# Branch A of an encoder layer: head outputs stored by SyncE, and both merge portions behind a step's second scores

## The chip, the cores and the metric

One core of one Trainium2 chip runs the whole layer. The metric is device time in microseconds for one execution. The kernel before takes 1680.21 us, the median of three runs from 1679.45 to 1682.18.

## The reference, cut to what matters

There are 1280 tokens of 1024 features in float32: a sample of 1024 and a prompt of 256, which do not attend to each other. A projection gives queries, keys and values of two attention branches, and gate logits. Branch A has eight query heads over two key heads and a window of 128 to either side, with a sink in the softmax. Branch B has twelve heads in three groups of dilation 1, 4 and 16, and merges the groups per head by the softmax over their log-sums:

```python
outs.append(_from_residues(o, dil))
lses.append(_from_residues(lse, dil))
alpha = jax.nn.softmax(jnp.stack(lses), axis=0)
o = jnp.sum(alpha[..., None] * jnp.stack(outs).astype(jnp.float32), axis=0)
...
merged = gates[:, :, 0] * (o_a.reshape(b, S, A_Q) @ w_branch_a) + gates[:, :, 1] * (o_b @ w_branch_b)
x = x + merged @ w_out
h = _rmsnorm(x, g_mlp)
return x + jnp.square(jax.nn.relu(h @ w_up)) @ w_down
```

## The kernel before, in words

Large products run on TensorE (PE) as three passes of split float32 operands (`mm3`, L192, and the schemes that use L347). The stages follow each other: projection with branch B's attention beside it, branch A's attention, the gated products of the branches, the output projection, the MLP.

The change lies in branch A's stage, which is written for a manual schedule: each engine executes its instructions in the order in which the code issues them. It works on 4 units (`u`, two heads each) of 10 token tiles (`t`, 128 rows). `order` lists the 40 pairs of unit and tile, and the loop at L1426 takes two of them at each step, so `j` runs 0, 2, ..., 40. A step holds, in this order:

- `values_of` for the pair of tiles of two steps ago: PE multiplies values by probabilities into the one bank `pv` (L1205), VectorE (DVE) copies it to a tile `o` (L1208), of which there are **two buffers**, and the tile is stored to a DRAM scratch `scr_o` (L1209).
- `transposes` of the last step's probabilities: PE (L1189), evicted by ScalarE (ACT, L272) and DVE (L274).
- `scores` of the first tile: PE writes both heads into the two `sc` banks (L1163, L1164), DVE adds the bias and takes the maximum (L1165, then L1169). One portion of `fill`. The exponential of both heads on ACT (L1175).
- `scores` of the second tile, two portions of `fill`, and its exponential.

`fill` is the generator `logits`: PE's gate-logit products of the projection, which have nothing to do with attention. Its results go through ACT to a tile `gs` (L1230) and by a store of SyncE (SP) to DRAM (L1231). A cycle of it takes five steps, which is ten tiles, so that steps whose `j` differ by ten hold the same widths of tiles and the same products.

`merges` is the generator `merge`: the softmax over branch B's groups. Its **first portion** (before the loop) transposes the log-sums, stores them to DRAM and loads them back in another layout: 25 small DMAs, all issued by GpSimd (POOL; L1260 and L1277). Portions two to five are empty. **Portion six**, in the step with `j = 8`, is seven DVE instructions (L1283 to L1290). Portion seven is one exponential on ACT (L1292). **Portion eight**, with `j = 10`, is nine DVE instructions (L1294 to L1307) and six DMAs of POOL (L1310). Portion nine is empty, ten and eleven issue loads `r` on SP, three DMAs each (one L1326, two L1329), and each of the last eighteen issues one such load, two items ahead, and the products of its own item on POOL (L1345, L1348).

Two kinds of queue matter. POOL executes its DMA issues in order among its products. SP does nothing but issue DMAs, in order: an issue waits for what fills or frees its tile, and, since the program gives SP's DMAs eight completion semaphores in turn, for the landing of the DMA eight issues before it. SP's other DMAs here are the loads of the next unit (`kk`, `kp`, `q`, `qp`: L429 to L447), weights (`raw`, L222), the stores of `gs`, and after the loop the gates `sg` (L1479) and the stored heads (L1386).

Of the kernel before, what the change touches and what calls it, by code (L numbers as in the profile page):

```python
# [97 lines left out]
def encoder_kernel(  # L98
# [5 lines left out]
    nc = tc.nc  # L104
# [31 lines left out]
    def bank(tag, name=None):  # L136
        return psum.tile([P, 512], F32, name=name or tag, tag=tag, bufs={"mm": 3, "sc": 2, "pt": 2, "pv": 1}[tag])
# [81 lines left out]
    def fetch():  # L219
        src, shape, _ = specs[len(raws)]  # L220
        raws.append(wslot("raw", shape))
        nc.sync.dma_start(raws[-1], src)  # L222
# [58 lines left out]
    scr_o = [dram.tile([P, 4, 2, P], F32, name=f"scr_o{t}") for t in range(0, NT, 2)]  # L281
# [41 lines left out]
    def steps_of(gen, n):  # L323
        for _ in range(n):
            next(gen, None)
# [93 lines left out]
    def load_unit(u):  # L419

        st = {}
        g = u // 2
        if u == 0:
            shared["kp"] = slot("kp", (P, 4, NP), F32R)
        if u % 2 == 0:
            kk = [slot("kk", (P, NS), F32R) for _ in range(2)]
            for i in range(2):
                for r in HALVES:
                    nc.sync.dma_start(kk[i][r, :].bitcast(F32), scr_ka[g, i, :, :NS])  # L429
                    nc.sync.dma_start(shared["kp"][r, 2 * g + i, :].bitcast(F32), scr_ka[g, i, :, NS:])  # L430
            shared["k"] = [Pair(kk[i], shared["kp"][:, 2 * g + i, :]) for i in range(2)]
        st["q"] = [Pair(slot("q", (P, NS), F32R), None) for _ in range(2)]
        for h in range(2):
            nc.sync.dma_start(st["q"][h].s.bitcast(F32), scr_qa[u][h].rearrange("a d t -> (a d) t")[:, :NS])
        if u:
            load_prompt(u, st)
        else:
            shared["v"] = [slot("va", (P, 8, P)), None]
            nc.sync.dma_start(shared["v"][0],
                              scr_v[:NS, 512 : 512 + P].rearrange("(t p) c -> p t c", p=P))  # L440
        st["k"], st["v"] = shared["k"], shared["v"]
        return st
# [9 lines left out]
    def load_bias(u, make):  # L452
        b = make("bias", (P, 2, 3 * P))
        nc.gpsimd.dma_start(b, toeplitz(0, 3 * P, -P, 2 * u))
        return b
# [26 lines left out]
    def attention_b(make):  # L482
# [148 lines left out]
        for j in range(0, n + 4, 2):  # L631
            load_v(j)
            load_v(j + 1)
            if j < n:
                scores(j)
            load(j + 3)
            if j > 2:
                pv = values_of(j - 4)
                store_values(j - 4, (nc.vector, nc.scalar)[j // 2 % 2], *pv)
            if j < n:  # L640
                biased(j)
            if 0 < j <= n:
                transposes(j - 2, nc.scalar)
            if j < n:
                biased(j + 1)
            if 0 < j <= n:
                transposes(j - 1, nc.vector)
            load(j + 4)
            if j < n:
                exponentials(j)  # L650
                exponentials(j + 1)
            yield
# [487 lines left out]
    if True:  # L1140
# [4 lines left out]
        def a3(name, shape=(P, 2, 3 * P), n=3, dt=F32):  # L1145
            return att.tile(list(shape), dt, name=name, tag=name, bufs=n)
# [8 lines left out]
        def scores(u, t):  # L1155
            st, bias = units[u]
            lo, W, c0 = tiles[t]
            s = a3("s", n=3)
            m = small.tile([P, 2], F32, name="m", tag="m")
            for h in range(2):  # L1160
                ps = bank("sc")
                q = st["q"][h][:, P * t : P * t + P]
                nc.tensor.matmul(ps[:, :W], q, st["k"][1][:, P * lo : P * lo + W], start=True, stop=False)  # L1163
                nc.tensor.matmul(ps[:, :W], q, st["k"][0][:, P * lo : P * lo + W], start=False, stop=True)  # L1164
                nc.vector.tensor_tensor_reduce(  # L1165
                    s[:, h, :W], ps[:, :W], bias[:, h, c0 : c0 + W], 1.0, -3.0e38,
                    op0=ALU.add, op1=ALU.max, accum_out=m[:, h : h + 1],
                )
            nc.vector.scalar_tensor_tensor(nm_a[:, 2 * u : 2 * u + 2, t], m, -1.0, nsink[:, 2 * u : 2 * u + 2],  # L1169
                                           op0=ALU.mult, op1=ALU.min)  # L1170
            live[u, t] = s

        def exponential(u, t, h):
            W, s = tiles[t][1], live[u, t]
            nc.scalar.activation(s[:, h, :W], s[:, h, :W], AF.Exp, bias=nm_a[:, 2 * u + h : 2 * u + h + 1, t],  # L1175
                                 accum_out=l_a[:, 2 * u + h : 2 * u + h + 1, t])

        def transposes(u, t):

            pt = a3("pt", (P, 12, P), 1)  # L1180
            jobs, at = [], []
            for i in range(2):
                at.append(len(jobs))
                jobs += [(live[u, t + i], b, h) for b in range(tiles[t + i][1] // P) for h in range(2)]
            for i, tag, eng in ((0, "pt", nc.scalar), (4, "pt", nc.vector), (8, "mm", nc.scalar)):
                if i < len(jobs):
                    ps, e = bank(tag, "pt"), min(len(jobs), i + 4)
                    for k, (s, b, h) in enumerate(jobs[i:e]):
                        nc.tensor.transpose(ps[:, P * k : P * k + P], s[:, h, P * b : P * b + P], ident)  # L1189
                    moved(eng, pt[:, i:e, :], ps[:, : P * (e - i)].rearrange("p (i q) -> p i q", q=P))  # L1190
            for i in range(2):
                live[u, t + i] = pt, at[i]

        def values_of(u, t):

            pv = bank("pv")
            for i in range(2):
                lo, W, _ = tiles[t + i]
                pt, at = live.pop((u, t + i))
                v, rest = units[u][0]["v"]  # L1200
                for b in range(W // P):
                    k = lo + b
                    src = v[:, k, HALVES[u // 2]] if k < 8 else rest[:, k - 8, HALVES[u // 2]]
                    for h in range(2):
                        nc.tensor.matmul(pv[HALVES[h], P * i : P * i + P], src, pt[:, at + 2 * b + h, :],  # L1205
                                         start=b == 0, stop=b == W // P - 1, skip_group_check=True)
            o = a3("o", (P, 2, P), 2)
            nc.vector.tensor_copy(o, pv[:, : 2 * P].rearrange("p (i q) -> p i q", i=2))  # L1208
            nc.gpsimd.dma_start(scr_o[t // 2][:, u], o)  # L1209

        def sums_a():

# [153 lines left out]
    if True:  # L1366
# [5 lines left out]
        def high_b(b):  # L1372

            ob_hi.block(b)
            ob_lo.block(b)
            nc.scalar.activation(ob_hi.t[b, 0], merged[b], AF.Copy)

        def low_b(b):
            nc.vector.tensor_tensor(ob_lo.t[b, 0], merged[b], ob_hi.t[b, 0].bitcast(F32), op=ALU.subtract)
# [3 lines left out]
        def load_o(t):  # L1383
            if t % 2 == 0:
                rows_o[t] = slot("o", (P, 4, 2, P))
                nc.sync.dma_start(rows_o[t], scr_o[t // 2])  # L1386
# [34 lines left out]
        n = len(order)  # L1421
        fill = logits()
        merges = merge()
        next(merges)
        steps_of(fill, 2)
        for j in range(0, n + 2, 2):  # L1426
            if j > 2:
                values_of(*order[j - 4])
                if j < n:
                    next(merges, None)  # L1430
            if j:
                transposes(*order[j - 2])
            if j < n:
                scores(*order[j])
                next(fill)
                for h in range(2):
                    exponential(*order[j], h)
                scores(*order[j + 1])
                steps_of(fill, 2)
                if j > 2:  # L1440
                    next(merges, None)
                for h in range(2):
                    exponential(*order[j + 1], h)
            else:
                steps_of(fill, 2)
                next(merges, None)
            if j == n - 4:
                high_b(0)
                low_b(0)
            if j < n and order[j][1] == 0 and order[j][0] < 3:  # L1450
                u = order[j][0] + 1
                units[u] = load_unit(u), load_bias(u, lambda name, shape: a3(name, shape, 2))
            if j in (n - 6, n - 4):
                fetch()
            if j == n - 2:
                load_o(0)
                load_o(1)
# [51 lines left out]
        for i, (x, b, c) in enumerate(jobs):  # L1509
            t0, n = BLOCKS[b]  # L1510
# [528 lines left out]
```

## Time and profile before

| | us |
|---|---|
| the profiled execution, its own time | 1681.2 |
| its span on the core | 1679.4 |
| median of the three runs | 1680.21 |
| PE busy | 1664.9 (99%) |
| DVE busy | 953.6 (57%) |
| ACT busy | 716.3 (43%) |
| POOL busy | 513.3 (31%) |
| granted TensorE clock, mean | 0.999 |

Times in the trace are microseconds from the start of the span. A row of a timeline gives the start, the duration, the engine, the line, the operation with its tiles and the count; in brackets stands how long the engine had been idle before it, and what ended that. Branch A's loop takes the time from about 539 to 677. A row of the DMAs gives the line's tiles, the issuing queue, the count, the KB of each and the median time from issue to landing. PE's busy share counts matmuls with overlapping, modelled ends; what tells of the loss is the idle time and the spacing of starts.

### The profile page before, as it was taken

To read this page: it belongs to the slowest core of one execution; us is meant where nothing else is said; L and a number is where in the kernel's file an instruction comes from. 1 tells how busy PE (TensorE), PEld (TensorE's weight loads), DVE (VectorE), ACT (ScalarE), POOL (GpSimd) and SP (SyncE) were. 2 spreads that over 40 slices of the span, in tenths; PEclk is the share of its full clock that TensorE was granted. 3 is DMA by queue.
4 is the path that set the end of the run, shared out by engine and by line. 5 is a ranking of instruction groups with operands and counts; after the bars stand their busy time and mean duration, and the time that the engine had idled before them with its cause. 6 is when DMAs were issued, how large, how long until landed. Compare 5 with 4: busy or idle time off the path is not lost. (4 is left out here: it accounts for less than half of the span.)

```text
span 1679.4 us, 24840 instructions
## 1 busy us (share of the span) xinstructions
PE 1664.9 (99%) x9268; PEld 1414.1 (84%) x9268; DVE 953.6 (57%) x1535; ACT 716.3 (43%) x1476; POOL 513.3 (31%) x400
## 2 busy tenths in 40 slices
PE   9999999999999999999999999999999999999998
PEld 7898888888888888888888888888888888888886
DVE  6732233445554565677278545545556775867665
ACT  6232323345654556654176333333334333333445
POOL 1312222111112473200100646546455250614240
PEclk9999999999999999999999999999999999999999
DMA  7416562666667693845121443443356934733333
GB/s 249 151 57 127 133 135 74 162 190 194 192 186 225 182 255 110 296 133 201 38 89 59 160 155 109 136 160 119 121 190 227 363 101 134 259 101 116 119 119 125
DMA packets 222360, 262.45 MB, mean 156 GB/s; under 512 B 29568, under 2 KB 151216, under 8 KB 222240
## 3 DMA queue, kind: packets, MB, share of 16 engines
q1 hardware_dynamic: 214080, 239.80, 45.1%
q0 software_dynamic: 7872, 20.54, 5.5%
q8 instruction: 73, 1.20, 0.3%
q10 hardware_dynamic: 288, 0.52, 0.1%
q14 instruction: 47, 0.39, 0.1%
HBM read 175.13 MB, written 90.92 MB: 158 GB/s over the span
## 5 line engine op out<-in xcount | busy, mean ns | idle before, releaser
L347 PE MATMUL dn<-dhi,ulo 128*128 128x512 f32 x448 | 174.5, 389 | 0.1
L347 PE MATMUL dn<-dlo,uhi 128*128 128x512 f32 x448 | 174.3, 389 | 0.0
L347 PE MATMUL dn<-dhi,uhi 128*128 128x512 f32 x448 | 174.3, 389 | 0.0
L347 PE MATMUL x<-chi,wlo 128*128 128x512 f32 x424 | 166.7, 393 | 0.2 <-ACT c L1953 0.2
L347 PE MATMUL x<-clo,whi 128*128 128x512 f32 x424 | 165.7, 391 | 0.1
L347 PE MATMUL x<-chi,whi 128*128 128x512 f32 x424 | 165.1, 389 | 0.0
L314 DVE TENSOR_TENSOR wlo<-ta,whi 128x1024 fp32r<-128x1024 f32 x30 | 55.8, 1861 | 171.5 <-ACT whi L312 171.5
L314 DVE TENSOR_TENSOR wlo<-raw,whi 128x1024 fp32r<-128x1024 f32 x60 | 89.1, 1485 | 103.5 <-ACT whi L312 101.4
L393 POOL TENSOR_TENSOR tb<-raw 128x512 f32<-128x512 f32 x25 | 32.6, 1304 | 364.4 <-DMA raw<-in_w_in_dram 129.0
L347 PEld LDWEIGHTS dn<-dhi,ulo 128*128 128x128 f32 x448 | 84.1, 188 | 18.2 <-DVE ulo L186 0.5
L347 PEld LDWEIGHTS dn<-dlo,uhi 128*128 128x128 f32 x448 | 84.1, 188 | 17.5
L347 PEld LDWEIGHTS dn<-dhi,uhi 128*128 128x128 f32 x448 | 84.1, 188 | 17.4
L347 PEld LDWEIGHTS x<-chi,whi 128*128 128x128 f32 x424 | 79.6, 188 | 16.9
L1733 POOL TENSOR_TENSOR t<-raw,t 128x1024 f32<-128x1024 f32 x16 | 46.3, 2915 | 155.3 <-DMA raw<-in_w_down_dram 155.3
L347 PEld LDWEIGHTS x<-chi,wlo 128*128 128x128 f32 x424 | 79.8, 188 | 15.7 <-ACT c L1953 0.6
L347 PEld LDWEIGHTS x<-clo,whi 128*128 128x128 f32 x424 | 79.8, 188 | 15.1 <-DVE clo L314 0.4
L186 DVE TENSOR_TENSOR ulo<-uraw,uhi 128x1024 fp32r<-128x1024 f32 x56 | 88.5, 1602 | 3.5 <-ACT uhi L185 3.5
L1882 DVE TENSOR_TENSOR v<-v,dn 128x512 f32<-128x512 f32 x90 | 59.4, 682 | 41.2 <-PE dn L347 41.2
L1982 POOL TENSOR_TENSOR u<-u,u 128x640 f32<-128x640 f32 x16 | 25.1, 1568 | 173.0 <-ACT u L1900 173.0
L186 DVE TENSOR_TENSOR dlo<-raw,dhi 128x1024 fp32r<-128x1024 f32 x32 | 49.1, 1558 | 46.5 <-ACT dhi L185 45.6
L347 PE MATMUL dn<-dhi,up 128*128 128x512 f32 x224 | 73.5, 389 | 0.0
L185 ACT ACTIVATE dhi<-raw 128x1024 fp32r<-128x1024 f32 x32 | 33.5, 1058 | 92.8 <-PE dn L347 92.4
(325 smaller groups left out, 4685.0 us busy)
## 6 DMA issues: line engine op xcount, KB each, us to landing
scr_u<-u SPq DMA_DIRECT2D x112, 320.0 KB, 2.6
uraw<-scr_u SPq DMA_DIRECT2D x56, 512.0 KB, 4.3
raw<-in_w_down_dram SPq DMA_DIRECT2D x36, 512.0 KB, 6.1
raw<-in_w_up_dram SPq DMA_DIRECT2D x32, 512.0 KB, 5.4
raw<-in_w_in_dram SPq DMA_DIRECT2D x25, 512.0 KB, 5.1
sg<-scr_g SPq DMA_DIRECT2D x32, 256.0 KB, 6.3
uraw<-scr_u SPq DMA_DIRECT2D x28, 256.0 KB, 4.5
qk<-scr_kb SPq DMA_DIRECT2D x48, 128.0 KB, 2.9
```

Source lines behind the costliest of these rows:

```text
L185: nc.scalar.activation(hi, src, AF.Copy)
L186: nc.vector.tensor_tensor(lo, src, hi.bitcast(F32), op=ALU.subtract)
L314: nc.vector.tensor_tensor(lo, src, hi.bitcast(F32), op=ALU.subtract)
L347: nc.tensor.matmul(ps, a, b, start=first and i == 0, stop=last and i == len(seq) - 1, skip_group_check=True)
L393: (nc.vector if vector else nc.gpsimd).tensor_tensor(o, x, y, op=ALU.subtract)
L1733: nc.gpsimd.tensor_tensor(o, a, b, op=ALU.subtract)
L1882: nc.vector.tensor_tensor(v, v, ps, op=ALU.add)
L1982: nc.gpsimd.tensor_tensor(u[S1], u21, u22, op=ALU.add)
```

## The change

The store of a pair's output goes from POOL's queue to SP's. A merge portion no longer stands between `values_of` and `transposes`; both portions of a step now stand behind the second scores and their two portions of `fill`, ahead of the second exponential. Numbers and sizes of instructions stay as they were.

```diff
             o = a3("o", (P, 2, P), 2)
             nc.vector.tensor_copy(o, pv[:, : 2 * P].rearrange("p (i q) -> p i q", i=2))
-            nc.gpsimd.dma_start(scr_o[t // 2][:, u], o)
+            nc.sync.dma_start(scr_o[t // 2][:, u], o)
...
             if j > 2:
                 values_of(*order[j - 4])
-                if j < n:
-                    next(merges, None)
             if j:
                 transposes(*order[j - 2])
...
                 steps_of(fill, 2)
                 if j > 2:
-                    next(merges, None)
+                    steps_of(merges, 2)
                 for h in range(2):
                     exponential(*order[j + 1], h)
```

On DVE, at the step with `j = 8`: before, the seven instructions of portion six (those on `cb`) follow the copy of the output and stand ahead of the eviction `pt` and of all of the step's scores (`s,m<-sc,bias`).

```order
L1169 SCALAR_TENSOR_TENSOR nm_a<-m,nsink 128x2
L1208 COPY o<-pv 128x256
L1283 COPY cb<-cb 128x2x32
L1283 COPY cb<-cb 128x2x8
L1283 COPY cb<-cb 128x2x32
L1283 COPY cb<-cb 128x2x8
L1288 TENSOR_TENSOR cb<-cb 128x40
L1289 TENSOR_TENSOR cb<-cb 128x40
L1290 TENSOR_TENSOR cb<-cb 128x120
L274 COPY pt<-pt 128x512
L1165 ISA s,m<-sc,bias 128x256
```

In the changed kernel the same seven follow the second tile's scores, and the next instruction is the copy of the next step's output.

```order
L1165 ISA s,m<-sc,bias 128x256
L1165 ISA m 128x1
L1169 SCALAR_TENSOR_TENSOR nm_a<-m,nsink 128x2
L1283 COPY cb<-cb 128x2x32
L1283 COPY cb<-cb 128x2x8
L1283 COPY cb<-cb 128x2x32
L1283 COPY cb<-cb 128x2x8
L1288 TENSOR_TENSOR cb<-cb 128x40
L1289 TENSOR_TENSOR cb<-cb 128x40
L1290 TENSOR_TENSOR cb<-cb 128x120
L1208 COPY o<-pv 128x256
L274 COPY pt<-pt 128x512
```

So they moved past the eviction and all of the step's scores. Portion eight moves in the same way one step later.

On POOL, between the first portion's loads and portion eight's stores (`scr_c`), the first four output stores are gone; `bias` is the next unit's bias.

```order
 L1277 DMA cb<-scr_n 128x2x4 x2
 L454 DMA bias<-wide_1311 128x2x384
-L1209 DMA scr_o_91<-o 128x256
-L1209 DMA scr_o_92<-o 128x256
-L1209 DMA scr_o_93<-o 128x256
-L1209 DMA scr_o_94<-o 128x256
 L1310 DMA scr_c<-cb 128x32
```

Before, the first of them could only be issued when POOL was through with all of the first portion.

On SP, behind the third unit's queries (`q`, `qp`), where the merge's loads `r` begin: the stores of outputs five and six (`scr_o_95`, then `scr_o_91` of the next unit) now stand among the loads, and the stores of `gs` come ahead of a step's loads.

```order
 L434 DMA q<-scr_qa_114 128x1024 x2
 L447 DMA qp<-scr_qa_114 128x256 x2
+L1209 DMA scr_o_95<-o 128x256
+L1231 DMA scr_g_141<-gs 128x512
 L1326 DMA r<-scr_b_83 128x512
 L1329 DMA r<-scr_c 64x512 x2
-L1231 DMA scr_g_141<-gs 128x512
 L1326 DMA r<-scr_b_85 128x4x128
 L1329 DMA r<-scr_c 64x4x128 x2
+L1209 DMA scr_o_91<-o 128x256
+L1231 DMA scr_g_141<-gs 128x256
```

Every output store is now one of the DMAs that SP's eight semaphores count.

## The prediction

> **What bounds the kernel now.** The page comes first: which engine is full.
>
> ```profile
> PE 1664.9 (99%) x9268; PEld 1414.1 (84%) x9268; DVE 953.6 (57%) x1535; ACT 716.3 (43%) x1476; POOL 513.3 (31%) x400
> ```
>
> PE is idle for 14 us of 1679 at most, so a change that takes no work from PE can only win where PE waits. The second view is the waits of PE between 530 and 700, which takes in branch A's stage; it has one row.
>
> ```profile
> PE sc L1163 <- DVE m L1165: 2.6, 2, 1.8
> ```
>
> Two waits, 2.6 us in all, and both are for DVE to free a bank `sc`. PE's timeline shows where: at 566.9 to 568.8 (step `j = 8`) and at 575.1 to 575.8 (step `j = 10`), ahead of the second scores of the very steps that hold portions six and eight of the merge.
>
> ```profile
> 568.75 0.38 PE L1163 MATMUL sc<-kp,qp 128*128 128x256 f32 x1 [1.84 <-DVE m L1165]
> ...
> 575.83 0.44 PE L1163 MATMUL sc<-kk,q 128*128 128x384 f32 x1 [0.74 <-DVE m L1165]
> ```
>
> DVE's timeline tells why DVE was late.
>
> ```profile
> 557.46 0.42 DVE L1208 COPY o<-pv 128x256 f32<-128x256 f32 x1 [0.27 <-PE pv L1205]
> ...
> 566.26 0.42 DVE L1208 COPY o<-pv 128x256 f32<-128x256 f32 x1 [4.52 <-DMA scr_o<-o]
> 566.61 0.50 DVE L1283 COPY cb<-cb 128x64 f32<-128x64 f32 x4
> ...
> 567.68 0.68 DVE L274 COPY pt<-pt 128x512 f32<-128x512 f32 x1
> ...
> 573.07 0.27 DVE L1294 TENSOR_TENSOR cb<-cb 128x120 f32<-128x120 f32 x1
> ...
> 574.75 0.68 DVE L274 COPY pt<-pt 128x512 f32<-128x512 f32 x1
> ...
> 579.72 0.42 DVE L1208 COPY o<-pv 128x256 f32<-128x256 f32 x1 [2.00 <-PE pv L1205]
> ...
> 593.57 0.42 DVE L1208 COPY o<-pv 128x256 f32<-128x256 f32 x1 [0.27 <-PE pv L1205]
> ...
> 600.43 0.42 DVE L1208 COPY o<-pv 128x256 f32<-128x256 f32 x1 [2.11 <-PE pv L1205]
> ...
> 612.71 0.42 DVE L1208 COPY o<-pv 128x256 f32<-128x256 f32 x1 [1.52 <-PE pv L1205]
> ```
>
> The third output's copy (566.26) does not wait for PE, as the others do, but for the landing of an earlier output's store: there are two buffers `o`, and the first store had not landed. Why not, POOL's timeline says.
>
> ```profile
> 555.51 6.06 POOL L1277 DMA_DIRECT2D cb<-scr_n  x8 [0.29 <-issue]
> ...
> 562.27 1.15 POOL L1209 DMA_DIRECT2D scr_o<-o  x2
> ```
>
> POOL issued the merge's small loads until 561.6 and only then the first two output stores, the first of which belongs to the copy one step ahead of that at 557.46. So the first stall is the store's place in POOL's queue plus portion six on DVE (566.61 to 567.68, 1.07 us); the second is portion eight alone (573.07 to 574.75, 1.68 us).
>
> **The change part by part.** *The two stalls.* What they cost is best read from equal work. Copies at 557.46 and 579.72 bracket the steps with `j` from 6 to 12; those at 593.57 and 612.71 bracket `j` from 16 to 22, with the same widths of tiles and the same pieces of `fill`. The first stretch takes 22.26 us, the second 19.14. The difference, **3.12 us**, is 0.54 more than the idle time of 1.84 + 0.74, because modelled ends hide part of a wait. I take 3.12.
>
> *The store.* On SP the first store can go when its copy is done, one step ahead of 557.46: nothing but a store of `gs` stands near it on SP. The third copy is due at 564.32 (557.46 plus 6.86, which is 600.43 - 593.57, the same step ten later), two steps after the first, and the longest landing quoted below, 10.9 us, is under two steps. So the wait of 4.52 goes. POOL's twenty issues of some 0.57 us (1.15 for two) go too; POOL is not waited for in the stage, so I count nothing.
>
> *Portion six behind the second scores.* DVE then has 1.07 us of it between the second maximum and the next copy, where DVE waits for PE anyway: the bracket of 2.00 at 579.72 is such a gap. But ACT's exponential of the merge and then the second tile's exponentials queue behind it.
>
> ```profile
> 571.43 0.50 ACT L1175 ACTIVATE s<-s,nm_a 128x256 f32<-128x256 f32 x1
> ```
> ```profile
> 572.61 1.09 PE L1189 MATMUL pt<-ident,s 128*128 128x128 f32 x8
> ```
>
> The second tile's exponentials end at 571.93 here, and would end at most 1.07 us later against PE, as if at 573.00. PE's eight transposes start at 572.61 and take the first tile's four first; at an eighth of 1.09 - about 0.12 - each, the fifth falls near 573.06. So it just holds, and costs nothing; without that cover, up to half a us.
>
> *Portion eight behind the second scores.* 1.68 us into a DVE gap of 2.00: nothing. Its six stores and all later loads `r` come up to a step later for POOL, whose products nobody in the stage waits for.
>
> *The stores among SP's loads.* This is the price. Here SP's loads are queued up, and each issue needs the landing of the one eight before. SP's timeline and the DMA view of 580 to 582 give both routes at the same moment:
>
> ```profile
> 580.52 0.32 SPq L1326 DMA_DIRECT2D r<-scr_b  x1
> ```
> ```profile
> r<-scr_b SPq DMA_DIRECT2D x1, 256.0 KB, 10.9
> ...
> scr_o<-o POOLq DMA_DIRECT2D x1, 128.0 KB, 9.1
> ```
>
> The store is the fifth output's, and took POOL 9.1 us. On SP, issued just ahead of the load at 580.52, it takes at most that load's 10.9 and lands by 591.4. The seventh copy needs that buffer: it stands at 593.57 now, and at 590.45 with the 3.12 gone. So it would be up to 0.95 us late. What DVE's lateness costs PE is read from the stalls: at `j = 10`, 1.68 us cost 0.74 of idle time and its part of the hidden 0.54, some 0.9; at `j = 8`, 1.94 (566.26 - 564.32) and 1.07 cost the other 2.2. Both leave **0.8 us of lateness free**. The bounds of this term: nothing (it lands as fast as POOL's did) to some 3 us (first rival). I take 0.2, near the lower end, since 0.95 - 0.8 is what the row of the same moment gives.
>
> At that moment POOL's route was 1.8 us quicker than SP's. The Trainium skill has a rule that speaks against the move: by "DMA: Bandwidth & Descriptors", section "Queues, rings and completion order", a data engine takes turns between the rows of queues that have work, so a store in POOL's own row need not stand behind SP's backlog, and one in SP's row must. The trace agrees in sign, by those 1.8 us; were the rule the whole story, the sum would be the first rival's.
>
> *After the loop.* The last stores now stand ahead of SP's loads of the gates.
>
> ```profile
> 676.64 0.42 DVE L1208 COPY o<-pv 128x256 f32<-128x256 f32 x1 [0.39 <-PE pv L1205]
> ```
> ```profile
> 679.84 1.34 ACT L1484 ACTIVATE sg<-sg,bg 128x512 f32<-128x512 f32 x2
> ...
> 687.07 0.60 ACT L1230 ACTIVATE gs<-mm 128x512 f32<-128x512 f32 x1 [3.92 <-PE mm L192]
> ```
> ```profile
> sg<-scr_g SPq DMA_DIRECT2D x7, 256.0 KB, 4.7
> ```
>
> The first gate can be loaded after the copy at 677.06, less 3.12: 673.9, plus an issue and 4.7 us, 679.1. The sigmoid stood at 679.84, less 3.12: 676.7. It is 2.4 us late, and ACT has 3.92 us idle before the third `gs`; no PE bank waits. Nothing; without cover, under 2.4.
>
> **The sum** against the profiled execution's own time: 1681.2 - 3.12 + 0.2 = 1678.3. The median of the runs shown lies 1.0 below that execution, so 1680.21 - 2.9 = **1677.3**. A measurement of this kernel tells about 0.2% from no change, 3.36 us: the forecast lies just inside it.
>
> **The rivals.** *Stores caught in SP's backlog.* If a store takes the 10.9 us of SP's fullest moment wherever the next unit's queries are loaded, the tenth store counts most. POOL's timeline, DVE's, and the landing of the tenth store:
>
> ```profile
> 616.87 0.56 POOL L1209 DMA_DIRECT2D scr_o<-o  x1
> ```
> ```profile
> 626.71 0.42 DVE L1208 COPY o<-pv 128x256 f32<-128x256 f32 x1 [0.21 <-PE pv L1205]
> ```
> ```profile
> DMA to landing us min/median/max: 7.5/7.5/7.5
> ```
>
> It lands at 616.87 + 10.9 = 627.8 in place of 624.4 (POOL's, 7.5); the twelfth copy, now 626.71, would be due at 623.6. That is 4.2 late, less 0.8: 3.4 us back at the worst, and 0.15 at the fifth. So between 1 us and all of the gain goes back: 1678 to 1680.5, at the middle 1679.3. For it: SP's landings grow where POOL's grow. Against it: POOL's own 7.5 us there already holds the backlog, and by it the store is only 0.8 late. Chance 0.22. (The rule of the Trainium skill named above would make this the rule.)
>
> *SP's queue falls behind, and the kernel is slower.* With eight landings outstanding and 10.9 us each, SP issues one DMA in 1.36 us. If SP is bound by this count and not by bytes, the six stores added from the fifth to the tenth put SP 8.2 us back: the tenth lands at 632.6, the twelfth copy is 9.0 late, PE 8.2, net 8.2 - 3.1 = 5.1 slower, 1685.3. It decides from where that store lands after 627.5 (623.6 + 0.8 + 3.1). Against it: the bytes are the same as before, and a backlog bound by bytes does not grow by their changing queue. Chance 0.08.
>
> *The second exponential is late at `j = 8`*, since its cover is under 0.1 us at the worst: up to half a us back beside the 0.2, 1677.8. Chance 0.08.
>
> *The wait was not the store's place*, and the third copy stays late: only portions six and eight are cured. Then 1.94 us of lateness less 0.8 stays, and 3.12 - 1.14 = 2.0 is won: 1678.2. Against it: the copy's own row names `scr_o<-o` as what ended its idle time. Chance 0.02.
>
> **How the numbers follow.** The forecast has the remaining 0.60; with the scatter of the runs (1679.45 to 1682.18) its own range is 1676 to 1678.5. The range for 8 in 10 is 1675.9 to 1681.0: it takes in the first rival and the late exponential and leaves out the slower one. Over 0.2% faster means below 1676.85: 0.45 of the forecast's cases and a few others, 0.30. Slower means above 1683.57: 0.09. Within: 0.61.
>
> **What would show it.** Right: in the changed profile the waits of PE for DVE in 530 to 700 are gone or under 0.5 us, no copy of an output names a store as its releaser, the stretch of `j` from 6 to 12 takes 19.1 to 19.4 us, as the next one. Wrong: a copy, the seventh or the twelfth first, that ends its idle time on `scr_o`; a transpose of PE at `j = 10` that waits for ACT; SP's loads of `r` later than before by several us.

## The result and the profile after

The changed kernel takes **1677.74 us**, the median of 21 runs (1675.61 to 1681.91), beside 1680.03 for the kernel before on the same chip (21 runs). The ratio is 0.9986, with a 95% interval of 0.998 to 0.9992: 2.3 us faster, inside the 0.2% of the forecast's "no change". The profiled execution has a span of 1676.1 us at a granted clock of 0.999.

The page of the changed kernel shows where the issues went: POOL is 16 us less busy, 11.2 of them for the twenty stores that it no longer issues, and nothing else differs by as much as 3 us.

```profile
PE 1663.5 (99%) x9268; PEld 1413.3 (84%) x9268; DVE 955.8 (57%) x1535; ACT 716.1 (43%) x1476; POOL 497.2 (30%) x380
```

PE's waits for other engines between 530 and 700:

```profile
PE sc L1163 <- DVE m L1165: 0.6, 1, 0.6
PE pt L1189 <- ACT s L1175: 0.2, 1, 0.2
```

Two waits are left, 0.8 us in all, in other places (at 626.5 and 609.3). DVE's timeline has the copies of the outputs again (start, duration, operation, in brackets the idle time before and what ended it), and one row (606.36) that stands ahead of a late copy:

```profile
556.30 0.42 DVE L1208 COPY o<-pv 128x256 f32<-128x256 f32 x1 [0.28 <-PE pv L1205]
563.17 0.42 DVE L1208 COPY o<-pv 128x256 f32<-128x256 f32 x1 [2.58 <-PE pv L1205]
...
575.43 0.42 DVE L1208 COPY o<-pv 128x256 f32<-128x256 f32 x1 [0.19 <-PE pv L1205]
...
606.36 1.48 DVE L1169 SCALAR_TENSOR_TENSOR nm_a<-m,nsink 128x2 f32<-128x2 f32 x1
608.41 0.42 DVE L1208 COPY o<-pv 128x256 f32<-128x256 f32 x1 [0.56 <-PE pv L1205]
...
615.61 0.42 DVE L1208 COPY o<-pv 128x256 f32<-128x256 f32 x1 [1.20 <-PE pv L1205]
...
624.94 0.42 DVE L1208 COPY o<-pv 128x256 f32<-128x256 f32 x1 [1.38 <-DMA scr_o<-o]
...
630.81 0.42 DVE L1208 COPY o<-pv 128x256 f32<-128x256 f32 x1 [1.68 <-PE pv L1205]
```

Counted from the first output of the stage, these are copies 2, 3, 5, 10, 11, 12 and 13. Three readings:

- **Both stalls are gone.** The third copy waits for PE, not for a store, and from the second to the fifth copy it takes 575.43 - 556.30 = 19.13 us, as in the undisturbed stretch; it was 22.26.
- **0.5 us goes at the eleventh copy.** From the tenth it takes 7.20 us; in the trace of before, the same two copies are 6.72 apart.
- **1.1 us goes at the twelfth.** From the eleventh to the thirteenth it takes 15.20; before, 14.14. The twelfth copy names a store.

Over the whole stage, from the second to the twentieth copy, that is 117.57 us in place of 119.18. I use this stage time below: it leaves out what lies ahead of the change, where profiled executions of all these kernels differ by over 1 us (the second copy starts between 555.9 and 557.8).

The twelfth copy's store is the tenth output's. SP's timeline, and its landing in the DMA view of 616 to 617 (count, KB, us to landing):

```profile
615.20 1.05 SPq L447 DMA_DIRECT2D qp<-scr_qa  x2
616.35 1.21 SPq L1209 DMA_DIRECT2D scr_o<-o  x1
```
```profile
scr_o<-o SPq DMA_DIRECT2D x1, 128.0 KB, 8.5
```

Its copy was done at 608.83. SP came to it 7.5 us later, behind loads `r` and the next unit's queries, and it took another 8.5 to land, at 624.85. The buffer was due at about 622.75 (7.14 us from the eleventh copy to the twelfth, as the run with three buffers below shows). In the kernel before, the tenth store landed at 624.40 and was due, by the same count, at 626.56: the copies have moved up by 3.8 us, and the landing has not.

The eleventh copy's loss is a chain of three engines. POOL's timeline and ACT's:

```profile
606.29 1.54 POOL L1348 TENSOR_TENSOR merged<-merged,r 128x512 f32<-128x512 f32 x1
```
```profile
607.94 0.62 ACT L1175 ACTIVATE s<-s,nm_a 128x384 f32<-128x384 f32 x1 [1.81 <-DVE nm_a L1169]
```

DVE's small instruction at 606.36, 0.16 us where nothing is in its way, ends at 607.84, and POOL's product ends at 607.83. The exponential starts then, and PE's transposes wait for it (the row `pt` above). I had no such thing in the prediction.

### The profile page after: what moved, and what is told of

Its sections match the earlier page's. It is cut to its first block, busy times and chain, and to the rows that moved or that the text cites. A ratio compares the mean times of both kernels' runs of the same rounds, so it can differ in the third digit from the quotient of the medians.

```text
span 1676.1 us, 24837 instructions
## 1 busy us (share of the span) xinstructions
PE 1663.5 (99%) x9268; PEld 1413.3 (84%) x9268; DVE 955.8 (57%) x1535; ACT 716.1 (43%) x1476; POOL 497.2 (30%) x380
## 5 line engine op out<-in xcount | busy, mean ns | idle before, releaser
L186 DVE TENSOR_TENSOR ulo<-uraw,uhi 128x1024 fp32r<-128x1024 f32 x56 | 92.1, 1666 | 3.5 <-ACT uhi L185 3.5
```

What stands on the lines that cost most here:

```text
L186: nc.vector.tensor_tensor(lo, src, hi.bitcast(F32), op=ALU.subtract)
```

## The experiments

Theories at this point: (a) each part takes its own stall away, with 0.8 us of lateness free in PE; (b) what goes back at the twelfth copy is the buffer's wait for the tenth store; (c) what goes at the eleventh is DVE held by POOL. Each kernel was timed beside the kernel before, on the same chip.

**The stores alone on SP**, portions as before:

```diff
-            nc.gpsimd.dma_start(scr_o[t // 2][:, u], o)
+            nc.sync.dma_start(scr_o[t // 2][:, u], o)
```

> Only the stores go to SyncE; the two portions of the merge stand where they stood before. If the two parts work apart, as the prediction has it, the third copy no longer waits for a store, but portion six (1.07 us) and portion eight (1.68 us) still stand ahead of their second scores: with 0.8 us of lateness free, PE loses 0.3 at j=8 and 0.9 at j=10, and the stretch of j from 6 to 12 takes 19.1 + 1.2 = 20.3 us in place of 22.3 before and 19.1 after. The later losses of the changed kernel stay (the twelfth copy waits for the tenth store, some 1.1 us): about 1 us faster than before in all. The rival that the portions alone made both stalls: the stretch stays near 22, and the kernel is no faster, or 1 us slower. The rival that the store alone made both: the stretch is 19.1.

1677.75 us, ratio 0.9987 (0.9978 to 0.9995). DVE's timeline:

```profile
556.73 0.42 DVE L1208 COPY o<-pv 128x256 f32<-128x256 f32 x1 [0.27 <-PE pv L1205]
563.59 0.42 DVE L1208 COPY o<-pv 128x256 f32<-128x256 f32 x1 [2.58 <-PE pv L1205]
570.05 0.42 DVE L1208 COPY o<-pv 128x256 f32<-128x256 f32 x1 [2.35 <-PE pv L1205]
577.05 0.42 DVE L1208 COPY o<-pv 128x256 f32<-128x256 f32 x1 [1.99 <-PE pv L1205]
```

The stretch is 20.32 us, as expected to 0.02. Its steps split it: 570.05 - 563.59 = 6.46 against 6.20 in the changed kernel (0.26 lost to portion six, 1.07 less 0.8), and 7.00 against 6.06 (0.94 lost to portion eight, 1.68 less 0.8). The expectation missed at the twelfth copy: nothing is lost there (13.99 from the eleventh to the thirteenth). The tenth store lands at 623.81, 1.0 us earlier than in the changed kernel, and PE is 1.1 us later and needs the buffer only at 623.9; the two together undo the loss. So that store's landing does not move along with PE, and what PE gains ahead of it uncovers it. What sets SP's time for it (issued at 615.91 here, at 616.35 there) no run shows.

**The portions alone**, stores on POOL. In the loop of the changed kernel only this is undone:

```diff
-            nc.sync.dma_start(scr_o[t // 2][:, u], o)
+            nc.gpsimd.dma_start(scr_o[t // 2][:, u], o)
```

> Only the two portions move behind the second scores; the stores stay on POOL. If the two parts work apart, the third copy still waits for the first store, 1.94 us late less 0.8 free, and the stall at j=10 is gone: the stretch of j from 6 to 12 takes 19.1 + 1.1 = 20.3 us, and nothing is given back at the twelfth copy: about 2 us faster than before. If the portions are all, the stretch takes 19.1 and the kernel is 3 us faster, more than the changed kernel; if the store's place is all, the stretch stays near 22 and the kernel is as before.

1677.97 us, 0.9987 (0.9979 to 0.9996).

```profile
556.67 0.42 DVE L1208 COPY o<-pv 128x256 f32<-128x256 f32 x1 [0.27 <-PE pv L1205]
564.57 0.42 DVE L1208 COPY o<-pv 128x256 f32<-128x256 f32 x1 [3.62 <-PE pt L1189]
...
576.01 0.42 DVE L1208 COPY o<-pv 128x256 f32<-128x256 f32 x1 [0.16 <-PE pv L1205]
```
```profile
560.62 0.59 POOL L1209 DMA_DIRECT2D scr_o<-o  x1
```

The third copy still waits for the first store (issued 560.62, landed 564.48). Its row names PE, but it starts 0.09 us after that landing, as the copies do whose rows name a store. It is 1.04 us late (due 556.67 + 6.86 = 563.53), not 1.94: POOL reached the store 3.95 us after the second copy here, 4.81 before. In the four other executions with the stores on POOL, with and without the portions' move, it is 4.0 to 5.1 us, so this difference need not be the move's doing. 1.04 less the 0.8 that is free leaves 0.2, and the stretch takes 19.34, not the 20.3 that was expected. So neither part needs the other to win most: the portions alone have a stage of 116.14 us, shorter than the changed kernel's.

**Three buffers `o`** in the changed kernel:

```diff
-            o = a3("o", (P, 2, P), 2)
+            o = a3("o", (P, 2, P), 3)
```

> The changed kernel with three buffers o in place of two. Theory: of the 3.1 us won, some 1.1 go back at the twelfth copy, which waits for the tenth store's landing behind the queries' loads on SyncE. With a third buffer that copy needs the ninth store, landed 12 us before: no copy names a store, the time from the eleventh to the thirteenth copy falls from 15.2 to 14.2 us (14.15 before the change), and the kernel is some 1 us faster than the changed one. Rival: that step is late because of the weights' low part on DVE just ahead of the copy, which waits for its own load, and not because of the store: the wait moves to another row and the time stays 15.2.

**1676.59 us**, 0.998 (0.9971 to 0.9989).

```profile
614.93 0.42 DVE L1208 COPY o<-pv 128x256 f32<-128x256 f32 x1 [2.05 <-PE pv L1205]
...
622.07 0.42 DVE L1208 COPY o<-pv 128x256 f32<-128x256 f32 x1
628.93 0.42 DVE L1208 COPY o<-pv 128x256 f32<-128x256 f32 x1 [2.57 <-PE pv L1205]
```

From the eleventh to the thirteenth it takes 14.00 us: 1.20 less than in the changed kernel. PE has no wait left between 530 and 700, and the stage takes 115.85. By itself this run does not settle the rival: the low part of the weights ends 7.11 us after the eleventh copy here and 7.95 in the changed kernel, where ACT made its high part later. Two runs below settle it: with the stores on ACT it ends at 7.86 and nothing is lost, and with one-input instructions at 6.85 and 0.73 is lost.

**The maximum by instructions of one input**, in the changed kernel with two buffers:

```diff
-            nc.vector.scalar_tensor_tensor(nm_a[:, 2 * u : 2 * u + 2, t], m, -1.0, nsink[:, 2 * u : 2 * u + 2],
-                                           op0=ALU.mult, op1=ALU.min)
+            for x in range(2):
+                nc.vector.tensor_scalar(nm_a[:, 2 * u + x : 2 * u + x + 1, t], m[:, x : x + 1], -1.0,
+                                        nsink[:, 2 * u + x : 2 * u + x + 1], op0=ALU.mult, op1=ALU.min)
```

> The changed kernel with the negated maximum written by two instructions (a tensor_scalar for each head, with one tensor input) in place of one scalar_tensor_tensor with two tensor inputs. Theory: half a us is lost between the tenth and the eleventh copy because that instruction on DVE is held until a product on POOL ends (its rows last 0.16 us or up to 1.5 us, and each long one ends with a row of POOL), and taking the stores off POOL has moved POOL's products onto it. With one tensor input it is not held: 80 rows of 0.1 to 0.2 us and none that ends with POOL's, the tenth to the eleventh copy takes 6.7 us in place of 7.2 (6.71 before the change), about 0.5 us faster than the changed kernel or somewhat more. Rival: the long rows are a wait for something else on DVE: the same share of the rows stays long, and the step stays 7.2. The twelfth copy's wait is as in the changed kernel by both.

1677.28 us, 0.9987 (0.9979 to 0.9995). The row of `nm_a` in the tile's view (count: ns minimum/median/maximum), first of the changed kernel, then of this one:

```profile
L1169 DVE SCALAR_TENSOR_TENSOR nm_a<-m,nsink x39: 161/164/1483, 541.3 to 667.5; 128x2 f32<-128x2 f32 x39
```
```profile
L1170 DVE TENSOR_SCALAR nm_a<-m,nsink x78: 203/207/211, 540.9 to 666.1; 128x1 f32<-128x1 f32 x78
```

With one tensor input no instruction is held, though 26 of them start within a product of POOL (14 of the two-input ones did); the tenth to the eleventh copy takes 6.72. Theory (c) holds as to what holds DVE. That the 0.5 us is a matter of which maximum is hit is seen below.

The run also parts the two causes at the twelfth copy. In the changed kernel POOL holds a maximum there too, so that (c) could have made that loss as well. Its row, and then the twelfth copy of this run, where nothing is held:

```profile
618.49 1.19 DVE L1169 SCALAR_TENSOR_TENSOR nm_a<-m,nsink 128x2 f32<-128x2 f32 x1
```
```profile
623.54 0.42 DVE L1209 COPY o<-pv 128x256 f32<-128x256 f32 x1 [1.98 <-DMA scr_o<-o]
```

The tenth store lands 8.73 us after the eleventh copy here, and 0.73 is lost (14.73 against 14.00); in the two profiles of the changed kernel it lands 9.24 and 9.15 after it, and 1.20 and 1.10 are lost. By these three, what lands beyond some 8.0 us is lost one for one, held maximum or not. So theory (b) holds.

**The kernel before with three buffers:** the edit of the third run, in the kernel before.

> The kernel before with three buffers o in place of two; stores and portions as before. If the first stall is the buffer's wait plus portion six, the third copy needs no store any more, and what is left is portion six (1.07 us less 0.8 free) and portion eight (1.68 less 0.8): the stretch of j from 6 to 12 takes 20.3 us, as with the stores alone on SyncE, the stage from the second to the twentieth copy 117.0 to 117.3 in place of 119.2, about 2 us faster than before. Rival: the store's place in POOL's queue costs in another way than by the buffer (POOL itself is late for something): the stretch stays near 22.

1678.79 us, 0.999 (0.9981 to 0.9999). The stretch is 20.32 us, the same as with the stores alone on SP. So what POOL's queue cost in the first stall was the buffer's wait and nothing else. The stage is 117.80, half a us over what was expected: between the eleventh and the thirteenth copy 0.72 is lost, and DVE's timeline, POOL's and PE's show theory (c) at another maximum:

```profile
614.53 1.57 DVE L1169 SCALAR_TENSOR_TENSOR nm_a<-m,nsink 128x2 f32<-128x2 f32 x1
```
```profile
614.78 1.28 POOL L1345 TENSOR_TENSOR r<-r 128x512 f32<-128x512 f32 x1
```
```profile
617.56 0.66 PE L1189 MATMUL pt<-ident,s 128*128 128x128 f32 x4 [0.27 <-ACT s L1175]
```

**Three buffers and one-input instructions** in the changed kernel:

> The changed kernel with three buffers o and the negated maximum by two instructions of one tensor input. With three buffers alone the stage from the second to the twentieth copy took 115.85 us and PE waited for nobody in it, so there is nothing more to win in the profiled execution: 115.8 us, and about the time with three buffers alone (1676.6), or up to half a us less, if in other executions POOL's products hold the maximum where it counts. Rival: the two instructions (0.41 us for 0.16) make DVE late somewhere: over 116.3 us.

1676.62 us, 0.9978 (0.9969 to 0.9986), stage 116.10. No gain over three buffers alone. 0.2 of the stage goes ahead of the fifth copy. DVE's timeline has portion six and the eviction behind it:

```profile
567.48 0.51 DVE L1284 COPY cb<-cb 128x64 f32<-128x64 f32 x4 [0.31 <-issue]
...
570.66 0.69 DVE L274 COPY pt<-pt 128x512 f32<-128x512 f32 x1 [0.88 <-ACT pt L272]
```

Portion six starts 4.32 us after the third copy here, 3.97 in the changed kernel. So the merge's exponential on ACT and the second tile's exponentials behind it are 0.26 us later than there, and ACT's eviction waits for them. This is the late second exponential that the prediction had as a rival; its cover, under 0.1 us by the prediction, is that small, since 0.26 us later costs 0.2. Why portion six starts late, with DVE idle for 0.31 us, the profile does not say.

**The same with the stores on POOL:**

> As the run before, but with the stores on POOL again: of the change only the portions' move is left, beside three buffers and the maximum by one-input instructions. If the queue of the stores matters only by when a buffer comes free, three buffers make it indifferent: the stage takes 115.8 us and the kernel as long as with the stores on SyncE, to half a us. If POOL's twenty issues of some 0.57 us cost something by themselves, it is slower by more than that; if SyncE's loads behind the stores do, it is faster.

1677.08 us, 0.9982 (0.9973 to 0.9991), stage 116.06: the same to 0.04 in the stage, 0.5 in the median, with the same 0.2 lost ahead of the fifth copy. With three buffers the stores' queue is indifferent within what was measured, and the twenty issues on POOL cost the stage nothing.

**The stores issued by ACT**, two buffers:

```diff
-            nc.sync.dma_start(scr_o[t // 2][:, u], o)
+            nc.scalar.dma_start(scr_o[t // 2][:, u], o)
```

> The changed kernel with two buffers, and the stores issued by ACT. They then stand in a row of queues that nothing else uses at that time. If a store is late because it stands behind SyncE's loads in their row, the fifth and tenth stores land 2 to 4 us after their issue, as stores do where little else moves, and the twelfth copy waits for none: the time from the eleventh to the thirteenth copy is 14.0 us. If it is late because all the data engines are full then, whatever the row, it lands 7 to 9 us after its issue, as it did on POOL (9.1 and 7.5 us) and on SyncE (9.5 and 8.5). ACT itself loses the issues, at least SyncE's 0.32 us each, and waits for the copy that a store needs; where that makes PE wait, the stage is slower than 117.6 us.

1677.06 us, 0.9982 (0.9973 to 0.9991), stage 115.84, no wait of PE. ACT's timeline has the tenth and the eleventh store; the DMA views of those moments give their landings:

```profile
608.99 0.33 ACTq L1209 DMA_DIRECT2D scr_o<-o  x1
615.71 0.35 ACTq L1209 DMA_DIRECT2D scr_o<-o  x1
```
```profile
scr_o<-o ACTq DMA_DIRECT2D x1, 128.0 KB, 5.5
...
scr_o<-o ACTq DMA_DIRECT2D x1, 128.0 KB, 6.7
```

The answer lies between the two theories: the fifth store took 4.5 us and the tenth 5.5. The tenth goes out the moment its copy is done, 7.4 us ahead of SP's 616.35, and that alone frees the buffer in time. Once the queries' loads are under way a row of its own helps little. A store issued between 614 and 617.5 took 6.7 us on ACT here and 6.0 in the last run below; 6.9 to 7.5 on POOL, in five executions; 7.1 to 8.5 on SP, in six. So most of the tenth store's lateness was SP's order of issue; of the landing, some 1 us was the row (POOL's range and SP's overlap), and the rest came whatever the row.

**The changed kernel once more:**

> The changed kernel once more, word for word, for a second profiled execution and for times beside the next run's. Theory: the twelfth copy's wait for the tenth store comes in every execution, since SyncE issues that store 7 us after its copy and it lands with the queries' loads: 1.0 to 1.2 us between the eleventh and the thirteenth copy above 14.0. The half us between the tenth and the eleventh copy is a matter of phase (a product of POOL may or may not lie across that maximum): 6.7 or 7.2. So the stage takes 117.0 to 117.6 us. Rival: both losses were of that one execution; then the stage takes 115.9 and the changed kernel is as fast as with three buffers.

1677.90 us, 0.9991 (0.9983 to 0.9999).

```profile
615.05 0.42 DVE L1208 COPY o<-pv 128x256 f32<-128x256 f32 x1 [1.00 <-PE pv L1205]
...
624.29 0.42 DVE L1208 COPY o<-pv 128x256 f32<-128x256 f32 x1 [1.09 <-PE sc L1164]
630.15 0.42 DVE L1208 COPY o<-pv 128x256 f32<-128x256 f32 x1 [1.84 <-PE pv L1205]
```

The loss at the twelfth copy is back, 15.10 us against 14.00 (the row puts its wait down to PE; the tenth store landed at 624.20). The loss at the eleventh is not: 6.72. So the first belongs to the kernel and the second to the phase between POOL and DVE, as far as two executions tell. Stage 116.99.

**The portions alone once more:**

> The portions alone (stores on POOL) once more, beside the changed kernel on the same chip. By the first profiles its stage is 1.4 us shorter than the changed kernel's (116.14 against 117.57), by the medians the two are equal. If the profiles stand for the rest, it is 0.5 to 1.4 us faster than the changed kernel here; if its first profile was a lucky one, the stage is longer this time, and the late place is the third copy (1.04 us late then, 0.2 lost) or the twelfth.

1677.87 us, 0.9985 (0.9977 to 0.9994), stage 116.62. The third copy is 1.13 us late this time and 0.3 is lost; another 0.36 goes behind the fourteenth copy, where a maximum at 633.44 is held for 1.92 us. By the stage it is still ahead of the changed kernel, by 0.4 to 1.4 us; by the medians (1677.97 and 1677.87 against 1677.74 and 1677.90) the two are equal. In the profiled executions the gain is lost outside the stage: the second copy starts at 556.67 and 557.82 with the portions alone, at 556.30 and 556.22 in the changed kernel, and what follows the twentieth copy takes 1002.5 us against 1002.1 to 1002.2. Whether this belongs to the kernels or to the executions, two of each do not tell.

**Stores on ACT and three buffers:**

> The changed kernel with the stores on ACT and three buffers o. With either alone the stage took 115.84 and 115.85 us and PE waited for nobody in it, so both together win nothing more: 115.8 us, 1676.5 to 1677. Rival: the twelfth copy, 0.6 us late with two buffers and the stores on ACT, costs something in other executions: then it is up to half a us faster than that kernel.

1677.32 us, 0.9985 (0.9976 to 0.9994), stage 116.37. Half a us is lost at the twelfth copy without any store: a maximum at 617.85 is held for 1.60 us, and the exponentials and the weights behind it are late. Nothing is won over either part alone.

Stage times beside the change of the median against the kernel before, timed on the same chip:

| kernel | stage, us | against before | median against before |
|---|---|---|---|
| before | 119.18 | | |
| changed, twice | 117.57, 116.99 | -1.6, -2.2 | -2.3, -2.3 |
| stores on SP alone | 117.06 | -2.1 | -2.3 |
| portions alone, twice | 116.14, 116.62 | -3.0, -2.6 | -2.1, -2.4 |
| before, three buffers | 117.80 | -1.4 | -1.5 |
| changed, one input | 116.54 | -2.6 | -2.8 |
| changed, three buffers | 115.85 | -3.3 | -3.4 |
| changed, three buffers, one input | 116.10 | -3.1 | -3.7 |
| the same, stores on POOL | 116.06 | -3.1 | -3.2 |
| changed, stores on ACT | 115.84 | -3.3 | -3.3 |
| the same, three buffers | 116.37 | -2.8 | -2.9 |

But for one execution of the portions alone the two columns agree to 0.7 us. The ratios' intervals are some 2 to 3 us wide, so the medians show that every kernel here is faster than the kernel before, and do not rank them; what ranks them is the stage, in one or two executions. Three buffers in the changed kernel, with and without one-input instructions, have the lowest medians, 1.1 us below the change as made, with intervals that overlap its own.

## Why the prediction was right, and where not

It said 1677.3 with a range of 1675.9 to 1681.0; 1677.74 came out. The gain was forecast as 2.9 us and measured as 2.3.

- *The two stalls, 3.12 us.* Right: 3.13 (22.26 to 19.13). The causes were those named: with one part undone, 20.32 or 19.34 remains.
- *0.8 us of lateness free.* Right: portion six (1.07) cost 0.26, portion eight (1.68) 0.94, a copy 1.04 late 0.2. At the twelfth copy it is about 1.0: 2.19 late cost 1.20, 2.10 cost 1.10.
- *Portion six behind the second scores, portion eight into DVE's gap, POOL's issues: nothing.* Right within the stage: with three buffers, or with the stores on ACT, 115.84 to 115.85 us and no wait of PE. The cover of portion six is thin, as it said: with one-input instructions and three buffers it gives way, for 0.2.
- *The stores among SP's loads, 0.2 at the seventh copy.* This is the step that failed, in place and in size. The fifth store did take 9.5 us, but SP issued it at 578.24, not at 580.5 (the prediction moved the copies up by 3.12 and left SP's load where it was), so it landed at 587.75, ahead of the copy at 589.29. The loss came at the twelfth copy, where the first rival had put it (chance 0.22): 1.1 to 1.2 us, not 0.2. That is the low end of that rival and not its 3.4, since the store took 8.5 us from SP, not 10.9. The prediction held against the rival that this store, landing at 624.4 for a copy due at 623.6, would be only 0.8 late. It landed at 624.85, and the buffer was due at 622.75, as the stage also began 1.2 us earlier in this execution. The rule of the Trainium skill that the prediction weighed ("DMA: Bandwidth & Descriptors", section "Queues, rings and completion order") agrees in sign: at that moment stores in rows of their own were on the mean 0.7 us (POOL) and 1.5 us (ACT) quicker than on SP. As the whole story it does not hold here, since 6.0 to 7.5 us remained in those rows.
- *After the loop: nothing.* Near enough: ACT waits 5.1 us for gates in all, and what follows the twentieth copy takes 1002.1 to 1002.2 us after the change, 1002.8 before; runs of the other kernels scatter from 1002.0 to 1003.1.
- *What was not in it:* DVE held by POOL, 0.5 us in one of two executions of the changed kernel.

The stage by its steps: 3.13 won, less 1.06 at the twelfth copy (15.20 against the 14.14 of before) and 0.48 at the eleventh, is 1.6, as the 119.18 and 117.57 have it. That the forecast's total came so near is in part luck: the stage lost some 0.9 us more to the stores than it had, and between the two profiled executions the time behind the stage fell by 0.6 us that it had at nothing. Of its signs of being right, the stretch came out; the waits of PE for DVE are 0.6 and 0.3 us in the two profiles, under its half us only in the second. Of its signs of error, one came true: a copy, the twelfth, names a store. Another came true in part: next to the tenth store SP's loads `r` start 1.1 to 2.6 us later than before, though no engine but POOL waits for them in the stage.

## What to carry to other kernels

When a stall goes, look for the next transfer whose landing does not come sooner with the engine that speeds up: it stays where it is, and the gain uncovers it. Before a store is moved to a queue of loads, read when that queue will issue it, not only how long it takes to land; another buffer made both indifferent here. And two changes that cure one stall each are worth trying apart: here either alone gave about the median of both.

## What the runs showed of the hardware that was not expected

DVE's negated maximum, an instruction with two inputs in SBUF, is held by a product of POOL until that product ends. In all ten profiled executions that have the two-input form, 9 to 12 of its 39 or 40 rows in the stage last over 0.25 us, up to 1.92 where 0.16 is the least, and each of those ends 16 to 31 ns after a product of POOL. Of 78 rows that start within one of POOL's DMA issues, 74 last 0.16. With one tensor input (three kernels) no row is over 0.22 us. The scores' instruction (L1165) has two tensor inputs, but one of them in PSUM: it starts some 300 times within a product of POOL, in all thirteen profiles, and no row of it is over 0.56 us, where 0.54 is the least of that width. The Trainium skill says so in "SBUF — State Buffer": a DVE instruction with two SBUF inputs contends with a GpSimd instruction that reads SBUF (section "Who interferes with whom"), and the second one to issue blocks fully until the first finishes (section "Summary: rules for kernel authors"). The runs agree that it contends and blocks. Who issued first is less plain: the other four start while POOL still issues a DMA, over 0.2 us ahead of its next product, and are held to that product's end, one of them through the product after it as well. Mostly the hold costs nothing; where the held maximum was the next thing PE needed, it cost 0.36 to 0.72 us, in four profiles.
